# Thirteen column units of a mixer projection in full fp32, with unsplit weights and tokens

## The chip, the cores and the metric

The kernel runs on one core of one Trainium2 chip. The metric is device time in microseconds (us) of one execution. Of the kernel before there are three timed runs, from 2965.73 to 2970.14 us with a median of 2966.01 us, and one profiled execution.

## The reference, cut to what matters

The program is two transformer blocks on one sequence of 256 tokens with model width 2048, everything in float32. The first block (a sparse attention, an RWKV-7 recurrence and a mixture of 16 experts) is touched by the change only in how some small parameters are loaded. The second block projects the normalised tokens to 12288 columns and feeds three mixers and three gates from them:

```python
h = rmsnorm(x, norm1_g[l])
proj = h @ w_in[l]
uv, s5_in = proj[..., :o_a], proj[..., o_a:o_b]          # 2048 and 1024 columns
qkv = proj[..., o_b:o_c]                                 # 3 x 1024 columns
gates = sigmoid(proj[..., o_c:].reshape(bsz, seq, 3, 2048) + b_gate[l])
y_a = gmlp_mixer(uv, ...)
y_b = s5_mixer(s5_in, ...)       # 64 groups of 16 channels, 64 complex states each,
                                 # s_t = a * s_(t-1) + B u_t, y = Re(C s) + d u, then a glu
y_c = stick_breaking_attention(q, k, v)      # 8 heads of 128
x = x + sum(gates * (ys @ w_branch)) @ w_out
x = x + square(relu(rmsnorm(x) @ w_mlp_in)) @ w_mlp_out
return rmsnorm(x, final_g)
```

## The kernel before, in words

**Products.** Weights come from memory in chunks of 512 KB (128 partitions x 1024 floats), issued by SP into one of three buffers `raw`. To multiply with nearly full precision at the fast rate, both factors are split into two fp32r parts: ACT copies a chunk into `wh` (L208), DVE subtracts that from the chunk into `wl` (L209), both in `load_split`. A *column unit* is 256 columns of a projection: `ws_steps` (L237) takes for each of the 16 slices of the model width and each half of 128 columns three matmuls into PSUM, wh by token-high, wh by token-low and wl by token-high (tiles `hx` in the trace), each with 256 tokens as the moving side. So such a unit has 96 matmuls, 4 chunks and 4 splits. Other units (W and V) have the tokens stationary, 512 columns moving, and are not touched.

**Order of the second block's mixers.** ORDER2 (L1478) lists the units: U and W are the two halves of the gated MLP, C the input of the state space mixer (S5), V and Q the attention (a Q unit is two column units, one of queries and one of keys), G the first gates, E the gelu of the S5 result. While PE goes through them, two generators are advanced: the S5 states (`rest`) each 3.9 us of planned matmul time, and the chains of gMLP and attention each 0.52. Within an engine a scheduler then fixes one order of all instructions; each engine works through its own queue in that order.

**The S5 states** are 32 steps i, four for each of eight tables. A step runs: PE makes the drive (`mx`); DVE multiplies it by cosine and sine tables (L1980, L1981, from PSUM), adds and subtracts (L1982, L1983), and scans two halves of 128 tokens for real and imaginary part (four L1993, with three small ops L1989 to L1991 between the halves); POOL multiplies the states back (L1995, L1996, into `b` and `z`); `result` subtracts and adds (L2003, L2004) on DVE if `i % 4 < CO`, else on POOL; ACT rounds to `sh` (L2007), POOL makes `sl` (L2008), and PE multiplies both with `C` into the result. POOL also builds the tables (L1948 to L1953, seven doublings each).

**After the S5 states** come the glu of its result (tiles `gs`), the branch products, the output projection and the MLP, all split products.

**Parameters.** `late_params` runs at the start of the expert stage: six rows of parameters are loaded by POOL's queue into a buffer of its own (`parl_r`) and transposed on PE (L176).

Of the kernel before, what the change touches and what calls it, by code (L numbers as in the profile page):

```python
# [10 lines left out]
F32 = mybir.dt.float32  # L11
# [3 lines left out]
OP = mybir.AluOpType  # L15
# [3 lines left out]
T = 256  # L19
D = 2048  # L20
KD = D // 128
EC = math.exp(-0.5)
LB = 3
WB = 1024
# [4 lines left out]
def _consts():  # L29
    p = np.arange(128)[:, None]  # L30
    f = np.arange(128)[None, :]
    t = np.arange(T)[None, :]
    c = {}
    c["ident"] = p == f
    c["bd64"] = (p // 64) == (f // 64)
    for d in (128, 64):
        half = d // 2
        inv = np.float32(10000.0) ** (-np.arange(half, dtype=np.float32) * np.float32(2.0 / d))
        ang = np.arange(T, dtype=np.float32)[:, None] * inv.astype(np.float32)[None, :]
        cos = np.cos(ang).astype(np.float32).T  # L40
# [12 lines left out]
    c["blk"] = (p // b) == (f // b)  # L53
    c["nsel"] = np.where(p % b == f[:, :b], -1.0, 0.0)
    c["iota"] = np.broadcast_to(f, (128, 128))
    c["before"] = p < f
    c["geq"] = p >= f
    c["strict"] = p < f
    c["tril"] = p >= f
    c["ntril"] = np.where(p >= f, -1.0e30, 0.0)  # L60
# [9 lines left out]
C2 = ("iota", "before")  # L70
C3 = ("geq", "strict", "tril", "ntril", "half", "odd")

# [43 lines left out]
class Ker:  # L116
    def __init__(self, tc, A, out, stack, dbg=None):
        self.tc, self.nc, self.A, self.out, self.dbg = tc, tc.nc, A, out, dbg or {}
        self.ctx = stack
        self.glob = self.pool("glob", 1)  # L120
        self.rawp = self.pool("raw", 3)
        self.whp = self.pool("wh", 3)
        self.slots, self.only, self.nraw, self.ahead, self.pending = None, None, 0, [], None
        self.par, self.done = None, set()
        self.sides, self.nmx = False, 0
# [35 lines left out]

    def param_rows(self, items, pool, name, q=None):
        nc = self.nc
        n = sum(i[2] for i in items)
        assert n <= 128
        r = pool.tile([128, 128], F32, name=name + "_r", tag="prow")
        nc.vector.memset(r, 0.0)
# [22 lines left out]
    def load_raw(self, parts, kn, cn):  # L190
        raw = self.raw_tile()
        rv = raw[:, :kn * cn].rearrange("p (k c) -> p k c", k=kn)
        for ap, c0 in parts:
            w = ap.shape[1]
            self.nc.sync.dma_start(rv[:, :, c0:c0 + w], ap.rearrange("(k p) c -> p k c", p=128))
        return raw

    def load_split(self, parts, kn, cn):
# [37 lines left out]

    def ws_steps(self, parts, cn, xh, xl, pieces, kn_chunk=4):  # L237

# [12 lines left out]
        for k0 in range(0, K, kn_chunk):  # L251
            h, l = self.load_split([(ap[k0 * 128:(k0 + kn_chunk) * 128], c) for ap, c in parts],
                                   kn_chunk, cn)
            for k in range(kn_chunk):
# [75 lines left out]
    def columns(self, x, g):  # L330
# [6 lines left out]
        def quarter(q):  # L337
            for k in range(4 * q, 4 * q + 4):
                ps = self.pmx()
                for b in range(2):  # L340
                    nc.tensor.transpose(ps[:, ts(b, 128)], x[:, b, ts(k, 128)], self.ident)  # L341
                nc.scalar.activation(hh[:, k], ps[:, :T], AF.Copy, scale=g[:, k:k + 1])  # L342
                nc.vector.scalar_tensor_tensor(hl[:, k], ps[:, :T], g[:, k:k + 1],
                                               hh[:, k].bitcast(F32), op0=OP.mult, op1=OP.subtract)
        self.hx = [hx[:, k].rearrange("p a t -> p (a t)") for k in range(KD)]
        return quarter, [hh[:, k] for k in range(KD)], [hl[:, k] for k in range(KD)]
# [97 lines left out]
    def late_params(self):  # L444

        A = self.A
        row = lambda n: A[n].rearrange("l (r c) -> (l r) c", c=128)
# [4 lines left out]
            ("b_glu", [(row("s5_b_glu_2"), 0, 0)], 8), ("s5_d", [(row("s5_d_2"), 0, 0)], 8),  # L452
            ("gm_g", [(row("gm_norm_g_2"), 0, 0)], 8)], self.glob, "parl")

# [697 lines left out]
    def moe(self):  # L1152
        nc, A, tc = self.nc, self.A, self.tc
        stt = nc.vector.scalar_tensor_tensor
        with ExitStack() as st:
# [20 lines left out]
            with ExitStack() as s2:  # L1176
                q = self.pool("rt", 1, stack=s2)
                wr = q.tile([128, KD, 20], F32, name="wr")
                nc.gpsimd.dma_start(wr[:, :, 0:4], A["w_route_group"][0].rearrange("(k p) c -> p k c", p=128))
                nc.gpsimd.dma_start(wr[:, :, 4:20], A["w_route_expert"][0].rearrange("(k p) c -> p k c", p=128))  # L1180
                br = q.tile([128, 20], F32, name="br")
# [293 lines left out]
    EARLY, XB, SB = (4, 2, 1)  # L1475
    LO, CO = (0, 2)
    PRE = (0,)
    RS, RC = (3.9, 0.52)  # L1478
    ORDER2 = ('U0', 'C0', 'C1', 'U1', 'U2', 'W0', 'C2', 'C3', 'W1', 'U3', 'GM', 'G0', 'V0', 'Q0', 'Q1', 'V1', 'Q2', 'Q3', 'G1', 'G2', 'E', 'G3')

    def block2(self):
# [3 lines left out]
        with ExitStack() as st:  # L1485
# [11 lines left out]
            def gate(d, pool, n, ci):  # L1497

                g = d[n, ci] = pool.tile([128, 512], F32, name="g")
                c0 = 6144 + 2048 * n + 256 * ci  # L1500
                v, bk = yield from self.ws_steps([(w_in[:, c0:c0 + 256], 0)], 256, hh, hl, two)
                nc.vector.tensor_mul(*(t.rearrange("p (a t) -> p a t", a=2) for t in (g, bk[0])), row)
# [31 lines left out]
            with ExitStack() as s2:  # L1534
                early, steps, chains = {}, {}, []
                vp = self.pool("vv", 1, stack=s2)
                steps.update(self.gmlp(y, w_in, vp, chains))
                steps.update(self.sb(y, w_in, vp, chains))
# [5 lines left out]
                cs = cc = 0.0  # L1544
                for n in self.ORDER2:
                    for t in steps[n]():
                        cs += t
# [11 lines left out]
                for ch in chains:  # L1559
                    for _ in ch:  # L1560
                        pass
            q = self.pool("br", 1, stack=st)
            gq = self.pool("gq", 2, stack=st)
# [68 lines left out]
    def gmlp(self, y, w_in, vp, chains):  # L1632
# [9 lines left out]
        def U(j):  # L1642
            if j == 0:
                nc.gpsimd.dma_start(ws, A["gm_w_s_2"][0].rearrange("g t s -> t g s"))
                nc.gpsimd.tensor_mul(ws, ws, c["tril"][:, None, :].to_broadcast([128, 8, 128]))
                nc.gpsimd.dma_start(bs, A["gm_b_s_2"][0][None].to_broadcast([128, 8, 128]))
            v, bk = yield from self.ws_steps([(w_in[:, ts(j, 256)], 0)], 256, hh, hl, two)
            yj = y[:, 2 * j:2 * j + 2]
# [46 lines left out]
    def sb(self, y, w_in, vp, chains):  # L1695
# [18 lines left out]
        def attend(j):  # L1714
# [4 lines left out]
            for i, (base, sc) in enumerate(((3072, 128 ** -0.5), (4096, 1.0))):  # L1719
                v, bk = yield from self.ws_steps([(w_in[:, base + 256 * j:base + 256 * (j + 1)], 0)], 256, hh, hl, two)  # L1720
                nc.vector.scalar_tensor_tensor(both[:, 2 * i:2 * i + 2], bk[0].rearrange("p (a t) -> p a t", a=2), sc,
                                               self.row, op0=OP.mult, op1=OP.mult)
            chains.append(heads(j, both[:, 0:2], both[:, 2:4], pre))

        def heads(j, q, k, pre):
# [15 lines left out]
            for i, w in enumerate(work):  # L1741
# [5 lines left out]
                nc.vector.tensor_sub(zs, zs, cs[:, :384])  # L1747
                nc.vector.tensor_add(dg(zs), dg(zs), b2(c["ntril"]))
                with self.tc.issue_after(pre):
# [40 lines left out]
    def s5(self, y, w_in, st):  # L1790
# [6 lines left out]
        with ExitStack() as s1:  # L1797
# [71 lines left out]
            pat = "(s a) n h -> (a n) s h"  # L1869
            nc.gpsimd.dma_start(br, A["s5_b_re_2"][0].rearrange(pat, a=2))  # L1870
            nc.gpsimd.dma_start(bi, A["s5_b_im_2"][0].rearrange(pat, a=2))
            kb = lambda k: sc[:, k][:, :, None].to_broadcast([128, 32, 16])
# [16 lines left out]
        def cols(j):  # L1889
            v, bk = yield from self.ws_steps([(w_in[:, 2048 + 256 * j:2304 + 256 * j], 0)], 256, hh, hl, two)  # L1890
            yj = y[:, 8 + 2 * j:10 + 2 * j]
# [270 lines left out]
```

## Time and profile before

| what | value |
|---|---|
| median of three runs | 2966.01 us |
| profiled execution | 2965.45 us |
| its span, first to last instruction | 2963.3 us |
| mean granted clock of TensorE | 0.988 of full speed |
| busy: PE, DVE, ACT, POOL | 96%, 71%, 54%, 15% of the span |
| instructions on PE, DVE, ACT, POOL | 17284, 2898, 2161, 623 |

The profiled execution stands for the median: it is 0.02% below it, and 2.2 us of it lie outside the span. The shares are averages over stages. PE is near full in most of the 40 slices of the page; the second block's mixers, with the S5 states, are the slices from about 1300 to 1770 us, and there alone POOL is busy.

### The profile page before, as it was taken

How to read it: one execution, taken by the hardware profiler on the slowest of the kernel's cores; microseconds unless marked ns; L12 is line 12 of the kernel's file. 1: busy time of each engine (PE TensorE's matmuls, PEld its weight loads, DVE VectorE, ACT ScalarE, POOL GpSimd, SP SyncE). 2: the span in 40 equal slices, each digit the busy share in tenths (PEclk: the TensorE clock that was granted, in tenths of full speed). 3: DMA queues.
4: the chain of work that ended last, by engine and by line, in shares of the span. 5: the costliest groups of instructions: out<-in, count | busy, mean ns of one | idle time of the engine just before them, and what ended most of it. 6: DMA issues, size and time to landing. Idle time of an engine off the chain costs nothing. (4 is left out here: it accounts for less than half of the span.)

```text
span 2963.3 us, 45262 instructions
## 1 busy us (share of the span) xinstructions
PE 2854.0 (96%) x17284; PEld 2508.5 (85%) x17284; DVE 2105.6 (71%) x2898; ACT 1613.5 (54%) x2161; POOL 456.4 (15%) x623
## 2 busy tenths in 40 slices
PE   8999999997999999998888889999999999999998
PEld 8998989876887788787777779999988888888887
DVE  7685876647898989887999987555555654456554
ACT  6456466546777777765444445444445553345443
POOL 1211111011000000017998840000000000000000
PEclk9999999998999999999999999999999999999999
DMA  6444443484989999854434336665556666666665
GB/s 196 131 116 122 116 117 104 128 288 154 371 289 348 378 370 354 313 169 145 125 114 121 100 107 193 185 186 185 183 184 196 190 188 194 194 187 190 190 194 171
DMA packets 400512, 576.77 MB, mean 195 GB/s; under 512 B 25032, under 2 KB 252624, under 8 KB 400160
## 3 DMA queue, kind: packets, MB, share of 16 engines
q1 hardware_dynamic: 397632, 567.74, 59.5%
q0 software_dynamic: 2624, 6.06, 0.8%
q8 instruction: 137, 2.24, 0.3%
q14 instruction: 87, 0.71, 0.1%
q10 hardware_dynamic: 32, 0.01, 0.0%
HBM read 571.64 MB, written 2.10 MB: 194 GB/s over the span
## 5 line engine op out<-in xcount | busy, mean ns | idle before, releaser
L209 DVE TENSOR_TENSOR wl<-raw,wh 128x1024 fp32r<-128x1024 f32 (+1 forms) x917 | 1135.1, 1241 | 631.2 <-ACT wh L208 618.8
L208 ACT ACTIVATE wh<-raw 128x1024 fp32r<-128x1024 f32 (+1 forms) x917 | 965.6, 1055 | 908.7 <-PE acc L218 717.1
L218 PE MATMUL acc<-hx,wh 128*128 128x256 f32 (+3 forms) x5280 | 1163.5, 310 | 0.2 <-ACT hx L342 0.2
L218 PEld LDWEIGHTS acc<-hx,wh 128*128 128x128 f32 (+2 forms) x5280 | 862.0, 192 | 55.2 <-issue 8.5
L218 PE MATMUL acc<-hx,wl 128*128 128x256 f32 x3152 | 896.1, 286 | 11.2 <-DVE wl L209 11.1
L218 PEld LDWEIGHTS acc<-hx,wl 128*128 128x128 f32 x3152 | 602.0, 191 | 22.0 <-DVE wl L209 13.0
L209 DVE TENSOR_TENSOR wl<-rx,wh 128x1024 fp32r<-128x1024 f32 x159 | 191.9, 1225 | 29.9 <-ACT wh L208 26.7
L218 PE MATMUL acc<-wl,xgh 128*128 128x512 f32 x512 | 203.6, 399 | 2.3 <-DVE wl L209 2.3
L218 PE MATMUL acc<-wh,xgh 128*128 128x512 f32 x512 | 202.4, 396 | 2.4 <-ACT wh L208 2.4
L218 PE MATMUL acc<-wh,xgl 128*128 128x512 f32 x512 | 202.4, 395 | 0.0
L208 ACT ACTIVATE wh<-rx 128x1024 fp32r<-128x1024 f32 x159 | 167.5, 1060 | 59.5 <-PE acc L218 33.0
L218 PE MATMUL acc<-wh,al 128*128 128x512 f32 x512 | 199.3, 389 | 0.0
L218 PE MATMUL acc<-wh,ah 128*128 128x512 f32 x512 | 199.2, 389 | 0.0
L218 PE MATMUL acc<-wl,ah 128*128 128x512 f32 x512 | 179.2, 389 | 0.0
L218 PE MATMUL mx<-wh,act 128*128 128x512 f32 x512 | 141.2, 395 | 1.5 <-DVE act L215 0.8
L218 PE MATMUL acc<-wh,hx 128*128 128x512 f32 x384 | 123.9, 407 | 0.0
L218 PEld LDWEIGHTS acc<-wl,xgh 128*128 128x128 f32 x512 | 96.2, 188 | 27.0 <-DVE wl L209 4.8
L218 PEld LDWEIGHTS acc<-wh,xgh 128*128 128x128 f32 x512 | 96.2, 188 | 24.6 <-ACT wh L208 3.6
L218 PEld LDWEIGHTS mx<-wh,act 128*128 128x128 f32 x512 | 95.8, 188 | 25.1 <-DVE act L215 1.2
L218 PEld LDWEIGHTS acc<-wh,xgl 128*128 128x128 f32 x512 | 96.1, 188 | 22.3
L218 PEld LDWEIGHTS acc<-wh,ah 128*128 128x128 f32 x512 | 96.1, 188 | 20.0
L218 PEld LDWEIGHTS acc<-wl,ah 128*128 128x128 f32 x512 | 96.2, 188 | 19.9
(589 smaller groups left out, 4150.9 us busy)
## 6 DMA issues: line engine op xcount, KB each, us to landing
raw<-in_w_in_dram SPq DMA_DIRECT2D x304, 512.0 KB, 3.7
raw<-in_w_mlp_in_dram SPq DMA_DIRECT2D x128, 512.0 KB, 3.8
raw<-in_w_mlp_out_dram SPq DMA_DIRECT2D x128, 512.0 KB, 4.6
raw<-in_w_e_gate_dram SPq DMA_DIRECT2D x80, 512.0 KB, 6.0
raw<-in_w_e_down_dram SPq DMA_DIRECT2D x77, 512.0 KB, 5.7
raw<-in_w_e_up_dram SPq DMA_DIRECT2D x75, 512.0 KB, 5.6
raw<-in_w_out_dram SPq DMA_DIRECT2D x57, 512.0 KB, 3.8
rx<-in_w_e_up_dram SPq DMA_DIRECT2D x53, 512.0 KB, 6.4
```

What stands on the lines that cost most here:

```text
L208: self.lasth = nc.scalar.activation(h[:, :n], raw[:, :n], AF.Copy).ins
L209: self.lastl = nc.vector.tensor_sub(l[:, :n], raw[:, :n], h[:, :n].bitcast(F32)).ins
L218: return self.nc.tensor.matmul(out, lhsT, rhs, start=start, stop=stop)
```

## The change

Nine names of ORDER2, thirteen column units in all, multiply the chunk as it was loaded by unsplit tokens, one fp32 matmul in place of three fp32r ones. The chunks go in turn into the buffers that were `raw`, `wh` and `wl`, and no ACT or DVE instruction touches them. The tokens `xf` (16 KB a partition) are made by four additions on POOL. The room is found by: a GpSimd descriptor room of 2048 bytes in place of the size that is set when nothing is said (a few DMAs on its queue are cut into pieces for it), two constants less, and the parameter rows of `late_params` in a `raw` buffer. CO goes from 2 to 4, so all 32 pairs of L2003 and L2004 are on DVE.

```diff
-C3 = ("geq", "strict", "tril", "ntril", "half", "odd")
+C3 = ("geq", "strict", "half", "odd")
...
+    def load_direct(self, parts, kn, cn):
+        self.nhome = (self.nhome + 1) % 3
+        t = (self.rawp if self.nhome == 0 else self.whp).tile([128, WB], F32, name=("raw", "wh", "wl")[self.nhome])
+        v = t[:, :kn * cn].rearrange("p (k c) -> p k c", k=kn)
+        for ap, c0 in parts:
+            w = ap.shape[1]
+            self.nc.sync.dma_start(v[:, :, c0:c0 + w], ap.rearrange("(k p) c -> p k c", p=128))
+        return v
...
+            if xf is not None:
+                w = self.load_direct(rows, kn_chunk, cn)
+                for k in range(kn_chunk):
+                    kk = k0 + k
+                    for i, (c0, m) in enumerate(pieces):
+                        self.mm(views[i], w[:, k, c0:c0 + m], xf[:, kk], start=kk == 0 and first[i],
+                                stop=kk == K - 1 and last[i])
+                    yield 0.43 * len(pieces)
+                continue
...
     def late_params(self):
+        rows = self.raw_tile()[:, :128]
...
-                nc.gpsimd.dma_start(wr[:, :, 0:4], A["w_route_group"][0].rearrange("(k p) c -> p k c", p=128))
-                nc.gpsimd.dma_start(wr[:, :, 4:20], A["w_route_expert"][0].rearrange("(k p) c -> p k c", p=128))
+                for k in (0, 8):
+                    for n, c0, c1 in (("group", 0, 4), ("expert", 4, 20)):
+                        nc.gpsimd.dma_start(wr[:, k:k + 8, c0:c1], A["w_route_" + n][0, k * 128:(k + 8) * 128]
...
-    LO, CO = (0, 2)
+    LO, CO = (0, 4)
+    DIRECT = ("U2", "C2", "C3", "U3", "Q0", "Q1", "Q2", "Q3", "G1")
...
+                full = self.pool("xf", 1, stack=s2).tile([128, KD, T], F32, name="xf")
+                for k in range(0, KD, 4):
+                    a, b = (self.hxt[:, k:k + 4, i].bitcast(F32) for i in range(2))
+                    nc.gpsimd.tensor_add(full[:, k:k + 4], a, b)
...
+                    self.xf = full if n in self.DIRECT else None
...
-                nc.vector.tensor_add(dg(zs), dg(zs), b2(c["ntril"]))
+                nc.vector.scalar_tensor_tensor(dg(zs), b2(c["geq"]), -1.0e30, dg(zs), op0=OP.mult, op1=OP.add)
...
-            nc.gpsimd.dma_start(br, A["s5_b_re_2"][0].rearrange(pat, a=2))
-            nc.gpsimd.dma_start(bi, A["s5_b_im_2"][0].rearrange(pat, a=2))
+            for s in range(0, 32, 8):
+                for t_, n in ((br, "re"), (bi, "im")):
+                    nc.gpsimd.dma_start(t_[:, s:s + 8], A[f"s5_b_{n}_2"][0, 2 * s:2 * s + 16].rearrange(pat, a=2))
...
-    nc = bacc.Bacc("TRN2", target_bir_lowering=False, num_devices=1)
+    nc = bacc.Bacc("TRN2", target_bir_lowering=False, num_devices=1, dynamic_dma_scratch_size=2048)
```

The scheduler orders the queues anew. First DVE, in the middle of the S5 scans, as it was before (`wl<-raw,wh` is a split, `z<-sc,a` a scan):

```order
L209 TENSOR_TENSOR wl<-raw,wh 128x1024
L215 TENSOR_TENSOR Bl_17378<-mx,Bh_17377 128x256
L1993 SCALAR_TENSOR_TENSOR z<-sc,a_17465 128x128 x2
L1993 SCALAR_TENSOR_TENSOR z<-sc,a_17313 128x128 x2
L209 TENSOR_TENSOR wl<-raw,wh 128x1024
L1938 TENSOR_TENSOR C_13630<-mx,C_13630 128x2x32 x2
L1989 SCALAR_TENSOR_TENSOR a_17465<-z,eh,a_17465 128x2
L1980 TENSOR_TENSOR a_17598<-mx,tab 128x512
L1981 TENSOR_TENSOR a_17599<-mx,tab 128x512
L1990 SCALAR_TENSOR_TENSOR a_17465<-z,eh,a_17465 128x1
L1991 SCALAR_TENSOR_TENSOR a_17465<-z,eh,a_17465 128x1
L209 TENSOR_TENSOR wl<-raw,wh 128x1024
```

And DVE near the end of the scans now (the lines of the S5 steps stand 30 lower in the file, L1980 is L2010):

```order
L2010 TENSOR_TENSOR a_17067<-mx,tab 128x512
L2011 TENSOR_TENSOR a_17068<-mx,tab 128x512
L2050 TENSOR_TENSOR y_13453<-y_13453,mx 64x256
L2020 SCALAR_TENSOR_TENSOR a_17012<-z,eh,a_17012 128x1
L2021 SCALAR_TENSOR_TENSOR a_17012<-z,eh,a_17012 128x1
L2012 TENSOR_TENSOR a_17067<-a_17067,a_17068 128x256
L2013 TENSOR_TENSOR a_17067<-a_17067,a_17068 128x256
L2023 SCALAR_TENSOR_TENSOR z<-sc,a_17012 128x128 x2
L2033 TENSOR_TENSOR b_16949<-b_16949,z 128x256
L2034 TENSOR_TENSOR b_16949<-b_16949,z 128x256
```

From the first scan to the last, 81 splits stood among them before and 29 stand there now; the pairs on `b` are all in this queue.

On PE, at the end of the S5 states, before, `mx<-sl,C` is the last product of the last step, and 93 more split matmuls like those behind it come before the glu:

```order
L218 MATMUL acc<-hx,wl 128x256
L218 MATMUL mx<-sl,C_13629 128x256
L218 MATMUL mx<-sh,C_13630 128x256
L218 MATMUL mx<-sl,C_13630 128x256
L218 MATMUL acc<-hx,wh 128x256 x2
L218 MATMUL acc<-hx,wl 128x256
```

And now, in the same place:

```order
L226 MATMUL mx<-sl,C_13645 128x256
L226 MATMUL mx<-sh,C_13646 128x256
L226 MATMUL mx<-sl,C_13646 128x256
L226 MATMUL acc<-xf,wh 128x256 x5
L226 MATMUL acc<-xf,wl 128x256 x8
L226 MATMUL acc<-xf,raw 128x256
L226 MATMUL mx<-zsb,cst_c_13438 128x256
```

Behind the last S5 product there now stand 29 fp32 matmuls, the rest of the last attention heads and 288 split matmuls (three units) before the glu begins; the S5 states end earlier in PE's order.

On PE, at the start of the expert stage, in the output projection of the first block (`yx`), now (`raw` is the buffer with the parameter rows):

```order
L226 MATMUL acc<-wh,yx 128x512
L226 MATMUL acc<-wl,yx 128x512
L174 MATMUL mx<-cst_cg,raw 128x128
L226 MATMUL acc<-wh,yx 128x512 x8
L226 MATMUL acc<-wl,yx 128x512
```

and before, further down the same projection:

```order
L218 MATMUL acc<-wl,yx 128x512
L218 MATMUL acc<-wh,yx 128x512 x2
L218 MATMUL acc<-wl,yx 128x512
L176 MATMUL mx<-cst_cg,parl_r 128x128
L1192 MATMUL mx<-cst_cg,xr 128x128 x2
L218 MATMUL acc<-wl,yx 128x512
```

The transposition of the parameter rows has moved up: twelve `yx` matmuls now stand between the last product of the recurrence (`PT,V`) and it.

## Rows read from the trace of the kernel before

**Rows 1.** The page's first part: busy time, share of the span, instructions.
```profile
PE 2854.0 (96%) x17284; PEld 2508.5 (85%) x17284; DVE 2105.6 (71%) x2898; ACT 1613.5 (54%) x2161; POOL 456.4 (15%) x623
```

**Rows 2.** A window behind the stage: start and end, length, busy time of each engine, PEclk, DMA, GB/s.
```profile
1800.00:1900.00 100.00, 100.00 (x843) 100.00 (x843) 58.40 (x60) 43.44 (x49) 0.00 (x0) 1.00 0.61 188
```

**Rows 3.** Windows by stage, from the third U unit to the last S5 result.
```profile
1332.00:1392.00 60.00, 53.95 (x344) 47.44 (x343) 44.86 (x88) 34.74 (x62) 48.54 (x99) 0.98 0.52 154
1392.00:1764.00 372.00, 316.56 (x2025) 283.00 (x2026) 351.48 (x575) 159.76 (x264) 304.63 (x389) 0.94 0.38 114
```

**Rows 4.** Waits of PE, 1392 to 1764: microseconds in total, times, longest.
```profile
PE mx L218 <- POOL sl L2008: 17.4, 13, 3.1
PE acc L218 <- DVE wl L209: 13.0, 7, 7.3
```

**Rows 5.** DVE by line, 1392 to 1764: count | busy, mean ns | idle before, releaser.
```profile
L209 DVE TENSOR_TENSOR wl<-raw,wh 128x1024 fp32r<-128x1024 f32 x80 | 115.9, 1451 | 4.9 <-ACT wh L208 4.7
L1993 DVE TENSOR_TENSOR_SCAN z<-sc,a 128x128 f32<-128x128 f32 x120 | 71.5, 632 | 0.1
L2004 DVE TENSOR_TENSOR b<-b,z 128x256 f32<-128x256 f32 x15 | 9.1, 608 | 0.0
L2003 DVE TENSOR_TENSOR b<-b,z 128x256 f32<-128x256 f32 x15 | 7.6, 504 | 9.1 <-POOL z L1996 9.1
```

**Rows 6.** POOL by line, the same stretch.
```profile
L2008 POOL TENSOR_TENSOR sl<-b,sh 128x512 fp32r<-128x512 f32 x32 | 48.0, 1501 | 22.3 <-ACT sh L2007 22.3
L2004 POOL TENSOR_TENSOR b<-b,z 128x256 f32<-128x256 f32 x16 | 16.9, 1058 | 0.0
L2003 POOL TENSOR_TENSOR b<-b,z 128x256 f32<-128x256 f32 x16 | 14.9, 933 | 1.1
```

**Rows 7.** DVE in order of time: start, microseconds, instruction.
```profile
1689.75 1.44 DVE L1993 TENSOR_TENSOR_SCAN z<-sc,a 128x128 f32<-128x128 f32 x1
1696.32 1.21 DVE L209 TENSOR_TENSOR wl<-raw,wh 128x1024 fp32r<-128x1024 f32 x1
1699.65 0.73 DVE L1993 TENSOR_TENSOR_SCAN z<-sc,a 128x128 f32<-128x128 f32 x2
```

**Rows 8.** PE in order of time, an fp32 pair and three fp32r products.
```profile
1578.33 0.89 PE L218 MATMUL mx<-sqk 128*128 128x256 f32 x4 [0.55 <-DVE a L1981]
1578.98 0.36 PE L218 MATMUL acc<-hx,wh 128*128 128x256 f32 x1
1579.18 0.28 PE L218 MATMUL acc<-hx,wl 128*128 128x256 f32 x1
1579.53 0.28 PE L218 MATMUL acc<-hx,wl 128*128 128x256 f32 x1
```

**Rows 9.** The last S5 product on PE, and the glu tiles' first matmul.
```profile
1765.33 0.28 PE L218 MATMUL mx<-sl,C 128*128 128x256 f32 x1
...
L218 PE MATMUL acc<-gs,wh x128: 276/279/331, 1776.6 to 1799.9; 128*128 128x256 f32 x128
```

**Rows 10.** POOL's parameter loads, a landing time (last column), and PE in that place.
```profile
605.33 0.56 POOL L145 DMA_DIRECT2D cst_c<-in_c_dram  x1 [88.08 <-ACT yx L214]
608.88 0.50 POOL L172 DMA_DIRECT2D parl_r<-in_gm_norm_g_dram  x1
...
parl_r<-in_gm_norm_g_dram POOLq DMA_DIRECT2D x1, 4.0 KB, 5.1
...
608.01 0.84 PE L218 MATMUL acc<-wh,yx 128*128 128x512 f32 x3
637.87 0.27 PE L176 MATMUL mx<-cst_cg,parl_r 128*128 128x128 f32 x1
```

**Rows 11.** A window after PE's longest wait in the S5 stretch.
```profile
1389.00:1403.00 14.00, 8.98 (x39) 8.43 (x39) 13.57 (x24) 4.57 (x9) 7.56 (x7) 0.51 0.38 108
```

**Rows 12.** POOL before the tables: the last long operation, and the wait behind it.
```profile
1295.59 2.40 POOL L1645 TENSOR_TENSOR gv<-gv,cst_c 128x1024 f32<-128x1024 f32 x1 [6.90 <-DMA gv<-in_gm_w_s_dram]
1341.26 0.95 POOL L1882 DMA_DIRECT2D cc<-in_s_c_re_dram  x1 [43.27 <-DVE eh L1865]
```

More of the change, by code (lines that the diff above doesn't have):

```diff
@@ L58, in _consts @@
     c["strict"] = p < f
-    c["tril"] = p >= f
-    c["ntril"] = np.where(p >= f, -1.0e30, 0.0)
     c["half"] = (p // 64) == np.arange(2)[None, :]
@@ L124, in __init__ @@
         self.par, self.done = None, set()
-        self.sides, self.nmx = False, 0
+        self.sides, self.nmx, self.nhome = False, 0, 0
         self.acc = self.pool("acc", 4, PSUM)
@@ L160, in pmx, with param_rows @@
         return self.mx.tile([128, 512], F32, name="mx", tag="mx", bufs=3)
-    def param_rows(self, items, pool, name, q=None):
+    def param_rows(self, items, pool, name, q=None, rows=None):
         nc = self.nc
@@ L165, in param_rows @@
         assert n <= 128
-        r = pool.tile([128, 128], F32, name=name + "_r", tag="prow")
+        r = pool.tile([128, 128], F32, name=name + "_r", tag="prow") if rows is None else rows
         nc.vector.memset(r, 0.0)
@@ L235, in ts_group, with ws_steps @@
         return self.whole(self.ts_steps(*args, **kw))
-    def ws_steps(self, parts, cn, xh, xl, pieces, kn_chunk=4):
+    def ws_steps(self, parts, cn, xh, xl, pieces, kn_chunk=4, xf=None):
         K = len(xh)
@@ L251, in ws_steps @@
         for k0 in range(0, K, kn_chunk):
-            h, l = self.load_split([(ap[k0 * 128:(k0 + kn_chunk) * 128], c) for ap, c in parts],
-                                   kn_chunk, cn)
+            rows = [(ap[k0 * 128:(k0 + kn_chunk) * 128], c) for ap, c in parts]
+            if xf is not None:
[7 more added lines that the diff above has]
+                continue
+            h, l = self.load_split(rows, kn_chunk, cn)
             for k in range(kn_chunk):
@@ L344, in quarter @@
                                                hh[:, k].bitcast(F32), op0=OP.mult, op1=OP.subtract)
+        self.hxt = hx
         self.hx = [hx[:, k].rearrange("p a t -> p (a t)") for k in range(KD)]
@@ L452, in late_params @@
             ("b_glu", [(row("s5_b_glu_2"), 0, 0)], 8), ("s5_d", [(row("s5_d_2"), 0, 0)], 8),
-            ("gm_g", [(row("gm_norm_g_2"), 0, 0)], 8)], self.glob, "parl")
+            ("gm_g", [(row("gm_norm_g_2"), 0, 0)], 8)], self.glob, "parl", rows=rows)
     def dump(self, name, t):
@@ L1178, in moe @@
                 wr = q.tile([128, KD, 20], F32, name="wr")
-                nc.gpsimd.dma_start(wr[:, :, 0:4], A["w_route_group"][0].rearrange("(k p) c -> p k c", p=128))
-                nc.gpsimd.dma_start(wr[:, :, 4:20], A["w_route_expert"][0].rearrange("(k p) c -> p k c", p=128))
+                for k in (0, 8):
+                    for n, c0, c1 in (("group", 0, 4), ("expert", 4, 20)):
+                        nc.gpsimd.dma_start(wr[:, k:k + 8, c0:c1], A["w_route_" + n][0, k * 128:(k + 8) * 128]
+                                            .rearrange("(k p) c -> p k c", p=128))
                 br = q.tile([128, 20], F32, name="br")
@@ L1500, in gate @@
                 c0 = 6144 + 2048 * n + 256 * ci
-                v, bk = yield from self.ws_steps([(w_in[:, c0:c0 + 256], 0)], 256, hh, hl, two)
+                v, bk = yield from self.ws_steps([(w_in[:, c0:c0 + 256], 0)], 256, hh, hl, two, xf=self.xf)
                 nc.vector.tensor_mul(*(t.rearrange("p (a t) -> p a t", a=2) for t in (g, bk[0])), row)
@@ L1561, in block2 @@
                         pass
+            self.xf = None
             q = self.pool("br", 1, stack=st)
@@ L1644, in U @@
                 nc.gpsimd.dma_start(ws, A["gm_w_s_2"][0].rearrange("g t s -> t g s"))
-                nc.gpsimd.tensor_mul(ws, ws, c["tril"][:, None, :].to_broadcast([128, 8, 128]))
+                nc.gpsimd.tensor_mul(ws, ws, c["geq"][:, None, :].to_broadcast([128, 8, 128]))
                 nc.gpsimd.dma_start(bs, A["gm_b_s_2"][0][None].to_broadcast([128, 8, 128]))
-            v, bk = yield from self.ws_steps([(w_in[:, ts(j, 256)], 0)], 256, hh, hl, two)
+            v, bk = yield from self.ws_steps([(w_in[:, ts(j, 256)], 0)], 256, hh, hl, two, xf=self.xf)
             yj = y[:, 2 * j:2 * j + 2]
@@ L1719, in attend @@
             for i, (base, sc) in enumerate(((3072, 128 ** -0.5), (4096, 1.0))):
-                v, bk = yield from self.ws_steps([(w_in[:, base + 256 * j:base + 256 * (j + 1)], 0)], 256, hh, hl, two)
+                v, bk = yield from self.ws_steps([(w_in[:, base + 256 * j:base + 256 * (j + 1)], 0)], 256, hh, hl, two, xf=self.xf)
                 nc.vector.scalar_tensor_tensor(both[:, 2 * i:2 * i + 2], bk[0].rearrange("p (a t) -> p a t", a=2), sc,
@@ L1889, in cols @@
         def cols(j):
-            v, bk = yield from self.ws_steps([(w_in[:, 2048 + 256 * j:2304 + 256 * j], 0)], 256, hh, hl, two)
+            v, bk = yield from self.ws_steps([(w_in[:, 2048 + 256 * j:2304 + 256 * j], 0)], 256, hh, hl, two, xf=self.xf)
             yj = y[:, 8 + 2 * j:10 + 2 * j]
```

## The prediction

> **What bounds the kernel now.** I read the page's first part, then windows, then the waits of PE in the windows that are not full, then the lines of DVE and POOL there. The first part shows PE busy 96% and DVE 71% of the span [rows 1]: as a mean, a PE-bound kernel. The windows show the exception. Behind the mixers PE is busy in 100 of 100 us and POOL in none [rows 2]; from 1392 to 1764, the 372 us in which the S5 scans run, PE is busy 316.6, DVE 351.5 (94.5%) and POOL 304.6 [rows 3]. There PE waits for `sl` (17.4 us, made by POOL) and for `wl` (13.0 us, made by DVE) [rows 4]: for the end of the S5 chain and for splits that queue on DVE among S5 operations. And its granted clock is 0.94 [rows 3], since after the longest of these waits, 7.3 us [rows 4], a window of 14 us ran at 0.51, the lower of the two levels [rows 11]. So DVE bounds this stretch, with POOL close, and PE the rest. I follow three sums: PE's work, DVE's work in the stretch, and what stands behind the stretch.
>
> **PE: dearer by about 33 us.** Thirteen units of 16 slices and two halves are 416 products of 256 columns. As three fp32r matmuls one costs 0.35 us: two `wl` matmuls one product apart start at 1579.18 and 1579.53 [rows 8]. An fp32 product's price stands just above: four records from 1578.33, the next matmul at 1578.98, 0.65 us [rows 8]. In that tile an fp32 matmul leaves two records, so these are one of 256 and one of 128 columns, and 256 columns cost 0.65 x 256/384 = 0.43 us. 416 x (0.43 - 0.35) = 33 us. By the start of the next fp32r record the bounds are 0.075 and 0.10 a product, 31 to 41 us. In a stretch that PE bounds this is lost; in one that DVE bounds it goes into PE's idle time, 372 - 317 = 55 us.
>
> The two passes of each fp32 product load weights twice, and the row says this is hidden, since the 0.65 us hold four loads as well [rows 8]. [...]
>
> **DVE: cheaper by about 57 us in the stretch.** 52 splits go, some three of them ahead of 1392; of 80 in the stretch I take 49 off. One costs 1.21 us where nothing disturbs it [rows 7] and 1.45 in the mean [rows 5]: 59 to 71 us; I take 71, since those left out were disturbed like the others. POOL's 32 operations of the pairs (16.9 + 14.9 us) [rows 6] come to DVE, where they cost 0.56 in the mean of the two lines [rows 5]: +18, or +13 at an undisturbed price of about 0.4. DVE's operations are long when POOL works beside them: a scan alone took 1.44 us, two together 0.73 [rows 7], and the mean is 0.632 [rows 5], so 120 scans lose 120 x 0.27 = 32 us. POOL's load falls from 305 to 273, a tenth, so I take 4 us off for this. DVE then has 351.5 - 71 + 18 - 4 = 294 us; at the same 94.5% the stretch takes 311 us and ends at 1703 in place of 1764. That is 10.0 us for each of 31 steps where it was 12.0. The bounds: at undisturbed prices throughout and all delays gone (-59, +13, -32) 274, so 290 us; with nothing gained, 372.
>
> [...]
>
> The stretch starts as before: its first operation waits for POOL's tables, and POOL for DVE's `eh` up to 1341 [rows 12]. The four additions for `xf`, 2.4 us each by POOL's operation of the same size, stand in the 43 us in which POOL waits there [rows 12], as do the eight pieces of `br` and `bi`. The first direct unit needs `xf` at about 1332; from 1298 there are 34 us for 10 us of work. If the smaller descriptor room makes each piece wait for the one before, 5 us each by a landing of that queue [rows 10], eight take 40 in place of a few, and `xf` is some 5 to 15 us late: a bound of +15, of which I take 0.
>
> **Behind the stretch PE has more left.** Before, 93 split matmuls stood between the last S5 product (1765.3) and the glu (1776.6) [rows 9]. Now 29 fp32 products (12.5 us), the last heads of the attention (2048 columns, 3.4 us, with their waits 7) and 288 split matmuls (288 x 0.118 = 34) stand there: 53.6 us. The last S5 product comes at 1704.5, the glu at 1758: 18.6 us earlier. A gain of 61 on DVE's side thus pays 19, since the PE work that used to fill the stretch now follows it. What is left from 1776.6 to the end is unchanged.
>
> **At the expert stage about 8 us are lost.** The parameter rows lie in a `raw` buffer now, and their transposition on PE stands twelve matmuls behind the end of the recurrence, in place of some 30 us later (637.87) [rows 10]. Twelve end at 608.0, where PE went on before. But POOL issues the loads from 605.33, since it waited there, the last at 608.88, and that one takes 5.1 us to land [rows 10]: 614. PE waits 6 us, with the whole projection behind it. A slow clock behind such a pause cost 14 x 0.49 = 7 us after 7.3 us [rows 11]; this one is shorter, and I take 2, between 0 and 7. Sum +8, from 0 (if the buffer and the loads are earlier) to 13.
>
> **The sum** from the profiled execution's 2965.45 us (0.02% under the median, so nothing is corrected): -18.6 + 8 = -10.6, so 2955 us. It is near break-even: with a stretch of 321 us in place of 311 nothing is gained.
>
> **The rivals.**
>
> *PE bounds the mixers.* If the chain no longer holds PE, the time from 1332 to 1776.6 is PE's work: 54 + 316.6 + 11.3 [rows 3, 9], 382 us busy of 444.6, plus 33 is 415; without waits the clock stays up, and the 6% of 372 us that it lacked are won back, 22 us: 393. The glu starts at 1725, 51 us earlier; with +8 it is 2922. If the clock does not come back, 2944. For it speaks that PE waits for `wl` in just the places where splits are gone now; against it, that each step's operations still go in turn through DVE, POOL, ACT and PE, and that POOL has 273 us of work.
>
> *The chain keeps its pace: slower.* If the 12.0 us of a step are the turn-around between DVE and POOL and not DVE's work, then fewer splits only leave DVE idle. Then the S5 states end at 1765 as now, 53.6 us follow, the glu is at 1819, and with +8 the time is 3016. In the trace 22.3 us of POOL's idle time ended with ACT's `sh` [rows 6] and 9.1 of DVE's with POOL's `z` [rows 5], which speaks for some turn-around; that DVE is 94.5% busy [rows 3] speaks against it. The price falls with each us that a step gets shorter: 31 steps at 10.35 us are break-even, above that it is slower.
>
> *Late tokens.* The pieces of `br` and `bi` wait for room, `xf` comes 15 us late, and PE stands still before the first direct unit and runs on at the lower clock: 2955 + 15 + 7 = 2977, about 0.4% slower than before. For it speaks only the landing time; against it the 34 us of room.
>
> *The direct loads don't hide.* That the transfers bound is excluded: the same bytes are loaded, at 114 GB/s in the stretch against 188 behind it [rows 2, 3].
>
> **How the numbers follow.** This kernel's runs can tell about 0.2%, 6 us, from no change. The forecast's own case (a stretch of 303 to 321 us) gets 0.45, from 2947 to 2965; PE-bound 0.22, from 2922 to 2947; the slower chain 0.23, from 2965 to 3016, most of it below 2985, since each us won on DVE counts; late tokens 0.10. Faster by over 0.2% (below 2960) is the second case and three quarters of the first: 0.56. Within 0.2% are a quarter of the first and a third of the third: 0.19. Slower, with the late tokens: 0.25. The range that leaves out 2 in 10 is 2922 to 2985; the forecast's own is 2947 to 2965.
>
> **What would show it.** In the changed profile: the fp32 products start 0.43 us apart; DVE's splits between the scans number about 31 and POOL has no `b` pairs; the stretch from the first to the last scan lasts about 311 us, with DVE over 90% busy; from the last `mx<-sl,C` to the first `gs` matmul pass some 54 us; PE waits about 6 us for a parameter load near 608; behind the glu nothing is different. Wrong would be: DVE below 85% in the stretch while its length stays over 321 (then the turn-around sets the pace), PE over 97% busy there (then PE bounds it), a wait of PE for `xf` near 1332, or fp32 products clearly above 0.43 us.

## The result

| kernel | median us | runs | ratio to before, 95% interval |
|---|---|---|---|
| before | 2965.87 (2964.49 to 2970.14) | 4 | |
| changed | 3008.86 (3003.53 to 3011.34) | 4 | 1.0139 (1.0122 to 1.0155) |

The change makes the kernel 43 us slower; 2955 us was forecast, from 2922 to 2985. The profiled execution of the changed kernel has a span of 3001.6 us, 38.3 us over before, and the comparison below is of these two executions.

The page's first part, against [rows 1]: DVE has 57 us less to do, as the change says, POOL 64 us less, and PE 30 us more.

```profile
PE 2883.9 (96%) x16868; PEld 2512.2 (84%) x16868; DVE 2049.0 (68%) x2878; ACT 1562.3 (52%) x2109; POOL 392.4 (13%) x603
```

To find where the time went I read the start of the same work in both traces. The columns after "before" and "changed" are the start of the instruction, and the last column is what was added since the line above.

| place | before | changed | added |
|---|---|---|---|
| end of the recurrence, first `yx` matmul behind it | 605.1 | 604.1 | -1.0 |
| first expert matmul (`acc<-wh,xgh`) | 695.0 | 724.8 | +30.8 |
| last expert matmul (`mx<-wh,act`) | 1273.4 | 1304.5 | +1.3 |
| first glu matmul (`acc<-gs,wh`) | 1776.6 | 1815.9 | +8.2 |
| end of the span | 2963.3 | 3001.6 | -1.0 |

So four fifths of the loss stand in the 90 us between the recurrence and the experts, where nothing is computed in another way, and the rest in the mixers, where 19 us less were forecast.

**Ahead of the experts.** PE in order of time (start, duration, instruction, idle time before it and what ended it), and ACT's first copy there:

```profile
608.95 0.63 PE L226 MATMUL acc<-wl,yx 128*128 128x512 f32 x1
612.83 0.42 PE L174 MATMUL mx<-cst_cg,raw 128*128 128x128 f32 x1 [3.25 <-DMA raw<-in_gm_norm_g_dram]
635.65 3.78 PE L226 MATMUL acc<-wh,yx 128*128 128x512 f32 x8 [22.40 <-ACT wh L216]
...
634.54 1.06 ACT L216 ACTIVATE wh<-raw 128x1024 fp32r<-128x1024 f32 x1 [29.88 <-DMA raw<-in_w_out_dram]
```

Where PE ran on before [rows 10], it now waits 3.25 us for the parameter rows and then 22.40 us for a copy of ACT, which had waited 29.88 us for a chunk of `w_out`. SP's queue shows why that chunk is late: first the changed kernel, then the one load that before has in between.

```profile
582.21 3.16 SPq L408 DMA_DIRECT2D raw<-in_x_dram  x2
603.61 0.37 SPq L193 DMA_DIRECT2D rx<-in_w_out_dram  x1
604.03 0.46 SPq L408 DMA_DIRECT2D rx<-in_x_dram  x1
604.54 3.33 SPq L193 DMA_DIRECT2D rx<-in_w_out_dram  x6
607.92 2.91 SPq L193 DMA_DIRECT2D raw<-in_w_out_dram  x2
611.22 0.85 SPq L408 DMA_DIRECT2D raw<-in_x_dram  x1
612.56 11.07 SPq L193 DMA_DIRECT2D raw<-in_w_out_dram  x8
```

```profile
584.94 0.37 SPq L195 DMA_DIRECT2D raw<-in_w_out_dram  x1
```

Before, the chunk was issued at 584.94, as soon as its buffer was free (a split on DVE ended at 584.92). Now the parameter rows lie in that buffer. In SP's order the load now stands behind eighteen others: it is the last of nineteen transfers from 603.61 on (the eighth of those from 612.56), and it waits for PE's transposition of the rows (`PE_49`):

```
before: L195 DMA raw<-in_w_out_dram 128x2x512 [waits DMAHW6_49,DVE_49]
changed: L193 DMA raw<-in_w_out_dram 128x2x512 [waits DMASW5_49,DMASW4_49,DMASW6_49,DMASW3_49,DMASW7_49,DMASW1_49,DMAHW3_49,DMASW0_49,PE_49]
```

It is issued near 623.6 (612.56 and 11.07), behind eighteen transfers of 512 KB, and ACT can begin at 634.54. The transposition itself had ended near 613.25 (612.83 and 0.42), some ten us before the load was issued: what makes the load late is its place in SP's order.

**In the mixers, ahead of the S5 steps.** POOL, DVE and PE at one time:

```profile
1344.82 9.37 POOL L1563 TENSOR_TENSOR xf<-hx 128x1024 f32<-128x1024 f32 x4
1354.15 2.33 POOL L1674 TENSOR_TENSOR gv<-gv,cst_c 128x1024 f32<-128x1024 f32 x1
...
1344.03 12.53 DVE L1812 TENSOR_SCALAR xmq<-xmq 32x128 f32<-32x128 f32 x1
...
1359.42 0.50 PE L1880 MATMUL mx<-cst_cg,pk 32*128 32x32 f32 x3 [8.84 <-DVE pk L1840]
```

A DVE instruction on 32x128 elements, 0.2 us elsewhere in the same line, lasts 12.53 us: from 1344.03 to 1356.56, until POOL is through the four additions for `xf` and one product (1344.82 to 1356.48). By its record it begins 0.79 us before the first addition, while POOL issues a load (1344.24 to 1344.80); whether that issue holds it too is not shown. What follows on DVE is late, and PE waits 8.84 us for it. Before, beside the product alone [rows 12] (1295.59 to 1297.99), an instruction whose line takes 0.16 us in the median lasted until 1298.01:

```profile
1296.04 1.97 DVE L1783 TENSOR_SCALAR xdq<-xdq 32x2 f32<-32x2 f32 x1
```

**In the S5 stretch.** The windows from the first `sl` to the last scans' results, to be held against [rows 3], and DVE and POOL by line in the first of them, against [rows 5, 6]:

```profile
1424.00:1747.00 323.00, 290.52 (x1401) 241.27 (x1400) 278.25 (x542) 99.83 (x194) 233.02 (x357) 0.96 0.36 111
1747.00:1816.00 69.00, 67.22 (x453) 63.21 (x452) 28.79 (x37) 32.12 (x51) 2.53 (x2) 1.00 0.40 123
```

```profile
L2023 DVE TENSOR_TENSOR_SCAN z<-sc,a 128x128 f32<-128x128 f32 x120 | 62.3, 562 | 0.1
L217 DVE TENSOR_TENSOR wl<-raw,wh 128x1024 fp32r<-128x1024 f32 x28 | 40.3, 1440 | 3.4 <-ACT wh L216 3.2 <-DVE xin L1930 0.2
L2010 DVE TENSOR_TENSOR a<-mx,tab 128x512 f32<-128x512 f32 x28 | 19.0, 679 | 9.0 <-PE mx L226 8.9
L2034 DVE TENSOR_TENSOR b<-b,z 128x256 f32<-128x256 f32 x32 | 22.1, 690 | 0.0
L2033 DVE TENSOR_TENSOR b<-b,z 128x256 f32<-128x256 f32 x32 | 18.1, 566 | 19.6 <-POOL z L2026 19.5
...
L2025 POOL TENSOR_TENSOR b<-z,tab 128x512 f32<-128x512 f32 x30 | 42.1, 1402 | 65.5 <-DVE z L2023 61.5 <-DVE a L2019 3.1 <-DVE vr L326 0.8
```

DVE's work fell somewhat further than forecast: 28 splits where 80 were (31 were forecast), all 32 pairs, 278 us busy (294 were forecast). But it is busy 86% of the stretch, not 94.5%. It waits 19.5 us for POOL's `z` (9.1 before [rows 5]), and now also 19.3 us in all for products of PE (8.9 of them in the line of L2010), where before there were 1.3. POOL waits 61.5 us for DVE's scans. From the first `b` of POOL to the last `z` pass 320 us (1419.4 to 1738.9), 370 before (1386.3 to 1756.7). PE is busy 90% of the stretch, 85% before [rows 3].

And behind it (PE, the last S5 product and the fp32 products after it; then the first glu matmul):

```profile
1759.65 0.28 PE L226 MATMUL mx<-sl,C 128*128 128x256 f32 x1
1759.77 2.32 PE L226 MATMUL acc<-xf,wh 128*128 128x256 f32 x10
1761.93 1.24 PE L226 MATMUL acc<-xf,wl 128*128 128x256 f32 x5
...
L226 PE MATMUL acc<-gs,wh x128: 279/280/282, 1815.9 to 1838.3; 128*128 128x256 f32 x128
```

From the last S5 product to the glu pass 56.3 us, where 53.6 were forecast and 11.3 stood before [rows 9]. Ten records, five fp32 products, take 2.16 us from 1759.77: 0.43 us each, as priced.

### The profile page after: what moved, and what is told of

It reads as the page before. It is cut to its first block, busy times and chain, and to the rows that moved or that the text cites. A ratio compares the mean times of both kernels' runs of the same rounds, so it can differ in the third digit from the quotient of the medians.

```text
span 3001.6 us, 44257 instructions
## 1 busy us (share of the span) xinstructions
PE 2883.9 (96%) x16868; PEld 2512.2 (84%) x16868; DVE 2049.0 (68%) x2878; ACT 1562.3 (52%) x2109; POOL 392.4 (13%) x603
## 4 chain that ended last, share of the span: by engine, by line
PE 46%; DVE 6%; POOL 4%; issue 1%; DMA 1%; ACT 0%; SPq 0%; ACTq 0%; DVEq 0%; POOLq 0%
PE acc L226 44%; PE mx L226 1%; DVE z L2023 1%; POOL b L2025 1%; POOL z L2026 1%; DVE xmq L1812 0%; POOL sl L2038 0%; POOL tab L1980 0%; DVE b L2034 0%; POOL ttmp L1979 0%; POOL tab L1978 0%; POOL tab L1981 0%; DVE wl L217 0%; POOL ttmp L1982 0%; POOL tab L1983 0%
## 5 line engine op out<-in xcount | busy, mean ns | idle before, releaser
L217 DVE TENSOR_TENSOR wl<-raw,wh 128x1024 fp32r<-128x1024 f32 (+1 forms) x865 | 1058.8, 1227 | 668.5 <-ACT wh L216 656.5
L216 ACT ACTIVATE wh<-raw 128x1024 fp32r<-128x1024 f32 (+1 forms) x865 | 911.0, 1055 | 939.3 <-PE acc L226 697.0
L226 PE MATMUL acc<-hx,wh 128*128 128x256 f32 (+3 forms) x4448 | 1000.6, 313 | 1.2 <-ACT wh L216 0.8
L226 PE MATMUL acc<-hx,wl 128*128 128x256 f32 x2736 | 773.0, 285 | 1.5 <-DVE wl L217 1.4
L226 PEld LDWEIGHTS acc<-hx,wh 128*128 128x128 f32 (+2 forms) x4448 | 724.9, 190 | 55.8 <-issue 8.0
L226 PEld LDWEIGHTS acc<-hx,wl 128*128 128x128 f32 x2736 | 518.7, 190 | 10.7 <-issue 4.5
L226 PEld LDWEIGHTS acc<-wh,al 128*128 128x128 f32 x512 | 96.1, 188 | 20.0
```

What stands on the lines that cost most here:

```text
L216: self.lasth = nc.scalar.activation(h[:, :n], raw[:, :n], AF.Copy).ins
L217: self.lastl = nc.vector.tensor_sub(l[:, :n], raw[:, :n], h[:, :n].bitcast(F32)).ins
L226: return self.nc.tensor.matmul(out, lhsT, rhs, start=start, stop=stop)
```

## The experiments

All times are medians, with the ratio to the kernel before as it ran on the same chip and its 95% interval. "Experts" is the start of the first expert matmul (695.0 before), "mixers" the time from the last expert matmul to the first glu matmul (503.2 before).

| kernel | us | ratio, interval | experts | mixers |
|---|---|---|---|---|
| changed | 3008.9 | 1.0139 (1.0122 to 1.0155) | 724.8 | 511.4 |
| rows moved | 2985.5 | 1.0070 (1.0053 to 1.0087) | 700.8 | 515.7 |
| additions on DVE | 2997.2 | 1.0113 (1.0096 to 1.0130) | 723.5 | 504.1 |
| br, bi by ACT | 3006.2 | 1.0142 (1.0126 to 1.0159) | 725.6 | 514.7 |
| rows moved, additions on DVE ("both") | 2972.3 | 1.0021 (1.0011 to 1.0030) | 701.9 | 504.0 |
| before, rows in `raw` | 2996.3 | 1.0107 (1.0091 to 1.0124) | 726.2 | 501.7 |
| both, no unit direct | 2973.4 | 1.0030 (1.0018 to 1.0041) | 700.9 | 501.2 |
| both, 4 units direct | 2967.8 | 1.0008 (0.9998 to 1.0018) | 700.7 | 498.6 |
| both, CO 2 | 2967.3 | 1.0007 (0.9997 to 1.0017) | 700.0 | 499.5 |
| both, CO 2, wr by ACT | 2971.1 | 1.0021 (1.0012 to 1.0030) | 704.6 | 499.8 |
| the same, 4 units direct | 2971.0 | 1.0016 (1.0007 to 1.0025) | 706.7 | 498.3 |
| rows in their own buffer, additions on DVE, CO 2 | 2961.9 | 0.9986 (0.9977 to 0.9995) | 696.5 | 499.4 |
| the same, 4 units direct | 2961.8 | 0.9987 (0.9978 to 0.9996) | 695.3 | 498.1 |

My theories: A, the raw buffer with the parameter rows is needed for the next chunk, and that costs the 30 us ahead of the experts; X, the POOL additions in a row hold up DVE; P, in the S5 stretch DVE and PE weigh about the same, so what fp32 takes from the one it gives to the other. The rivals: B, only the transposition waits; R, the small descriptor room makes the S5 parameters late; D, the relief of DVE is worth the forecast 19 us; N, fp32 only costs.

**The rows out of the raw buffer.**

```diff
-            self.late_params()
+            self.late_params(raw2.tile([128, WB], F32, name="raw")[:, :128])
```

> The changed kernel with the parameter rows in a buffer of the expert stage instead of a raw buffer. Theory A (the raw buffer with the rows is the one that the next chunk of the first block's output projection needs, so that chunk is loaded behind 17 others and PE waits 22 us for it, besides 3 us for the rows): the first expert matmul starts near 695 us as before, and the time falls by 28 to 33 us, from 3009 to about 2978. Rival B (what costs is only the transposition that waits for the rows, 3.2 us, and the slow clock behind it): it falls by at most 8 us, to about 3001.

The time fell by 23 us to 2985.5, less than the 28 to 33 that A gave, and the expert matmuls started at 700.8, not near 695. Both waits are gone, and the chunk was issued at 584.90 again. So A held for the waits, and B (at most 8 us) did not; 5 to 6 us of the loss stayed, which the last experiments take up.

**The same place in the kernel before.** One edit to it: `rows=self.raw_tile()[:, :128]` in `late_params`.

> The kernel before with one edit: the parameter rows in a raw buffer, as in the changed kernel. Theory A (the raw buffer with the rows is needed for the next chunk of the output projection): all of what this edit costs is in the first block's output projection, PE waits 20 us and more for a chunk near 613 us, and the time is 23 to 31 us above before, 2989 to 2997. Rival B (only the transposition waits): at most 8 us, 2974.

It cost 30.6 us. PE's waits from 600 to 700 (total, times, longest):

```profile
PE acc L218 <- ACT wh L208: 24.0, 1, 24.0
PE mx L176 <- DMA raw<-in_gm_norm_g_dram: 6.1, 1, 6.1
```

The wait for the transposition that I had priced is 6.1 us, as I had it; the wait for the chunk, which I had not, is 24.0 us.

**The additions on DVE.** `nc.vector.tensor_add` in place of `nc.gpsimd.tensor_add` for `xf`.

> The changed kernel with the four additions that make the unsplit tokens on DVE instead of POOL. Theory X (five long POOL operations in a row keep one small DVE instruction from 1344.0 to 1356.6, and PE waits 8.8 us behind it, then runs on a slow clock): no DVE instruction of the S5 parameters takes over 3 us, PE's wait near 1359 is gone, and the time falls by 9 to 14 us, to about 2997. Rival R (the S5 parameters are late since the eight pieces of br and bi wait for the small descriptor room, to 1340): the wait stays, and the time is within 3 us of 3009.

2997.2 us, 11.7 less, and PE is busy without a gap where it waited, at full clock. The last piece of `bi` is still issued only at 1338.89, so the late pieces that R names are there and the wait is not:

```profile
1330.00:1364.00 34.00, 34.00 (x279) 33.42 (x279) 28.83 (x84) 13.58 (x15) 7.15 (x6) 1.00 0.75 224
```

**br and bi by ACT's queue**, whole, in place of eight pieces that are issued 3.2 to 4.4 us apart.

```diff
-            for s in range(0, 32, 8):
-                for t_, n in ((br, "re"), (bi, "im")):
-                    nc.gpsimd.dma_start(t_[:, s:s + 8], ...)
+            nc.scalar.dma_start(br, A["s5_b_re_2"][0].rearrange(pat, a=2))
+            nc.scalar.dma_start(bi, A["s5_b_im_2"][0].rearrange(pat, a=2))
```

> The changed kernel with br and bi loaded whole by ACT's queue, not in eight pieces by POOL's. Rival R (the room makes them late): the wait of PE near 1359 is gone and the time falls by 9 to 14 us, to about 2997. Theory X: the POOL additions come some 25 us earlier but still stand in a row, one small DVE instruction still takes about 10 us beside them, and the time falls by 0 to 6 us, since the S5 chain may then be less late.

2.7 us less, which the spread of the runs (3003.5 to 3011.3 before the edit, 3005.8 to 3010.6 with it) cannot tell from nothing, so R fell here too. In detail it went another way than X had it: two additions and the product stand in a row, the other two additions each alone, and three DVE instructions last until the POOL operations beside them end, 5.33, 2.32 and 2.39 us. First POOL, then DVE:

```profile
1315.69 4.75 POOL L1563 TENSOR_TENSOR xf<-hx 128x1024 f32<-128x1024 f32 x2
1320.41 2.33 POOL L1674 TENSOR_TENSOR gv<-gv,cst_c 128x1024 f32<-128x1024 f32 x1
1327.20 3.35 POOL L1563 TENSOR_TENSOR xf<-hx 128x1024 f32<-128x1024 f32 x1 [4.45 <-DVE xdf L1808]
...
1317.56 5.33 DVE L1865 TENSOR_TENSOR den<-lre 32x128 f32<-32x128 f32 x1
1328.25 2.32 DVE L1809 TENSOR_SCALAR xdq<-xdf 32x2 f32<-32x2 f32 x1
```

PE's wait moved with them (5.7 us for a DVE `hx`). In all three kernels that were run with the additions on POOL, one of these small instructions was that long (12.53, 12.13 and 5.33 us).

**Both edits.**

> The changed kernel with both edits: rows in a buffer of the expert stage, and the additions on DVE. Theories A and X together: 28 to 33 and 9 to 14 us less, 2962 to 2972, about the time of the kernel before (2966). If only A is right about 2978, if only X about 2997, if neither over 3000.

2972.3 us: A and X together, 36.6 us, just past the end of what was expected. The mixers take 504.0 us, and 503.2 in the kernel before: with both waits mended, the 13 fp32 units and the 32 pairs on DVE together gain nothing.

**Both edits, and no unit direct** (`DIRECT = ()`).

> The changed kernel with the rows in a buffer of the expert stage and the additions on DVE (2972 us, as the run with both edits), and now with no unit direct: all 28 column units split, all 32 pairs of the S5 on DVE. What the fp32 products are worth by themselves. Theory P (DVE bounds the S5 stretch, and what the fp32 products take off it is given back by PE, whose work grows by 33 us): the S5 states end 40 us and more later, but only a few matmuls follow them, and the time is within 8 us of 2972. Rival D (DVE's relief is worth the forecast 19 us and something else lost it): 2985 to 2995. Rival N (the fp32 products only cost): below 2960.

2973.4 us, within 1.1 of the run with 13 units: P. The last S5 product comes 52 us later (500.1 us after the last expert matmul, 448.3 with 13 units, and 1.1 us ahead of the glu). The mixers as one window, with 13 units and with none:

```profile
1282.40:1786.40 504.00, 461.07 (x2497) 394.71 (x2496) 404.48 (x800) 188.43 (x350) 292.00 (x470) 0.97 0.42 127
```

```profile
1279.50:1780.70 501.20, 443.28 (x2913) 399.39 (x2913) 459.24 (x845) 233.38 (x389) 329.63 (x470) 0.95 0.43 128
```

DVE is busy 404 us in place of 459. PE is busy 461 in place of 443, and idle 43 in place of 58: 15 us less idle, 18 us more work (33 were priced at full clock; the granted clock is 0.97 with 13 units and 0.95 with none).

What DVE waits for between the first `b` and the last `z`, with 13 units (328.9 us, 1388.2 to 1717.1) and then with none (371.8 us, 1400.1 to 1771.9):

```profile
DVE b L2033 <- POOL z L2026: 15.5, 6, 5.4
DVE a L2010 <- PE mx L226: 9.7, 4, 4.7
DVE zsb L1776 <- PE mx L226: 7.3, 1, 7.3
```

```profile
DVE b L2033 <- POOL z L2026: 15.1, 9, 2.9
DVE y L2050 <- PE mx L226: 2.2, 1, 2.2
```

The waits for POOL are the same. Those for PE are 19.4 us in all with 13 units and 2.2 with none: the engine that was relieved now waits for the one that got the work. DVE is busy 87% of the stretch with 13 units, 94% with none. POOL's waits for DVE's scans are 59.0 and 56.0 us (32.2 in the kernel before), so they were there without a direct unit.

**4 of the 13 units direct**, DVE and PE between the two ends.

> As the run with both edits (2972 us), with only U2, C2, C3 and U3 direct, 4 units of 13. Theory P: PE's extra work falls from 33 to 10 us, DVE keeps 36 splits more than with 13 units, the stretch ends between the two, and the sum is better than either end if DVE and PE are about equally loaded: 2962 to 2972. Rival D: a part of the relief, 2978 to 2985.

2967.8 us, 4.5 better than 13 units, inside what P expected; PE is busy 443 us as with none. But the stretch does not end between the two: it is 375 us long (1385.0 to 1760.2), as with none, since 74 of the 80 splits are still in it. It only starts earlier, 106 us after the last expert matmul in place of 121.

**CO back at 2.**

> As the run with both edits (2972 us), with CO back at 2: half of the 32 pairs of subtractions and additions on POOL again. If DVE bounds the stretch with 13 units direct, 16 pairs at 0.63 us each, 20 us, come off DVE and POOL gets 32 us: a shorter stretch by up to 10 us, 2962 to 2972. If POOL or the turn-around between DVE and POOL sets the step, it is slower: 2975 to 2990.

2967.3 us: the 16 pairs on DVE cost 5.0 us. That was not asked in the prediction, which put them into DVE's sum. The time is where the first case had it, but its reason failed: the stretch is as long as with CO 4 (327.8 us for 328.9), DVE is busy in it 281 us for 285, and POOL 262 for 243. The second case, a step set by POOL or by the turn-around, asked for a slower kernel and failed too. What is gained stands behind the last S5 product (51.0 us to the glu in place of 55.7); why is not shown.

**The router weights by ACT's queue** (`nc.scalar.dma_start`, two pieces), on top of both edits and CO 2, with 13 and with 4 units:

> The changed kernel with rows in a buffer of the expert stage, additions on DVE, CO at 2, and the router weights wr loaded by ACT's queue in two pieces, not by POOL's in four that wait 6 us for each other. If the small descriptor room is what is left of the loss ahead of the experts (the first expert matmul at 700 us, at 695 before), that 5 us goes: 2961 to 2964, 2 to 5 us under before. If not, 2967 as without this edit.

> As e9_wr with only U2, C2, C3 and U3 direct. Theory P (DVE and PE weigh about the same in the S5 stretch; 13 units load PE by 33 us, 4 units by 10): between 2955 and 2964, at least as fast as with 13 units. If the relief of DVE counts for more, slower than with 13 units by 5 us.

Both times missed: 2971.1 us, 3.8 above the run without this edit, and 2971.0 (for 4 units with CO 2 no run without it was made). That 4 units are as fast as 13 held. The experts start later, not earlier; with 13 units there is a longer wait for a chunk of the projection at its end:

```profile
658.66 2.08 PE L226 MATMUL acc<-wh,yx 128*128 128x512 f32 x4 [4.15 <-ACT wh L216]
```

So taking the four pieces away did not bring the last 5 us back; the next runs do so with the four pieces in place. How the two transfers by ACT's queue delay that chunk was not tried.

**The rows in a buffer of their own**, as before the change; 64 bytes a partition were missing, and the descriptor room gave them (1984 bytes).

> As the run with both edits and CO at 2 (2967 us), but the parameter rows in a buffer of their own as in the kernel before (64 bytes of the descriptor room pay for what it lacks). Theory G (what is left of the loss ahead of the experts, the first expert matmul at 700 us against 695, is the buffer that the rows take from the ring of the expert stage, so that chunks of the projection come later): 694 to 697 us there, and 2961 to 2964. Rival W (the router weights in four pieces by POOL, 6 us apart): 2967 as before.

> As e11_own with only U2, C2, C3 and U3 direct, 4 units of 13: the mixers as with 4 units, which by theory P (DVE and PE about equally loaded) are within 4 us of 13 units: 2958 to 2966.

The experts start at 696.5 and 695.3, and the times are 2961.9 and 2961.8 us, the first 5.4 under the run with the rows in the expert stage's ring: G. These two are the only versions faster than the kernel before, by 0.14% (0.05 to 0.23%) and 0.13%, and whether 13 or 4 units are direct makes no difference that can be measured. Their mixers take 499.4 and 498.1 us, 503.2 before, so with CO at 2 the direct units may be worth some 4 us. A run with these edits and no unit direct was not made, so this is not shown.

## Why the prediction was wrong

**The loss ahead of the experts was mis-sized; this is the largest failure.** The step "Sum +8, from 0 ... to 13" counted PE's wait for the rows: six microseconds, and the kernel before with that one edit shows 6.1. It left out that the buffer has a next tenant. The same order of the queues that showed the transposition moved up shows that tenant's load behind eighteen others on SP, and the bound of 13 was worked out without looking at it. Measured: 30.6 us with the edit alone, 24.0 of them PE's wait for the next chunk.

**"Late tokens" was priced at nothing in the sum, and its mechanism was another one.** The prediction put the additions into POOL's idle time, and let PE wait for `xf` if they came late. PE never waited for `xf`: the additions end at 1354.15, and the first fp32 product starts at 1373.8. That POOL is idle says nothing on DVE, and the row that would have shown it stood in the trace: an instruction of DVE, 0.16 us in the median of its line, took 1.97 us beside the one POOL product in that place. Measured: 11.7 us, and 13.2 with the rows moved. The pieces that the rival named do come 3.2 to 4.4 us apart, the last at 1339.8, but the runs show no time that hangs on it. In the changed kernel's trace one DVE instruction, which by its record began 0.79 us before them, lasted 12.53 us, until five POOL operations in a row had ended.

**The S5 stretch: DVE's sum nearly held, its busy share did not.** 294 us of DVE work were forecast, and 275 (changed) and 285 (both edits) were measured from the first `b` to the last `z`. But the step "at the same 94.5%" failed: DVE is busy 86% and 87% of 320 and 329 us. The prediction kept DVE's idle share as it was, and put the 33 us of fp32 work into PE's idle time at no price. The runs with 13 units and with none show the price: DVE's waits for PE went from 2.2 to 19.4 us, while those for POOL stayed at 15. So it is not the turn-around between DVE and POOL that took what was missing. The sign that the prediction named for it (DVE below 85% with a length over 321) is not met in either kernel, and with CO back at 2 the stretch did not get longer, as it should have. In all kernels with 13 units the last `z` comes 433 to 440 us after the last expert matmul, whether the first `b` came 106 us after it (both edits: 434.7) or 115 (changed: 434.4). That points at PE's order of products as what sets the end. No run varied that order, so this stays argued.

In the terms of the forecast, the run with both edits against the kernel before: the stretch starts 7.1 us earlier and is 41.5 us shorter (61 were forecast), from its end to the last S5 product pass 5.0 us more (nothing was put there), and 44.4 us more PE work follows (42.3 were forecast). That is 0.8 us later at the glu, where 18.6 earlier were forecast. In the changed kernel, with the DVE instruction of 12.53 us, the four are +2.0, -50.9, +12.2 and +44.9, or 8.2 us later.

**PE's price and what follows the stretch held.** 0.43 us a product; the ten weight loads of the first five lie beside their matmuls (2.03 us from 1759.65, and the matmuls from 1759.77); 56 us behind the last S5 product for 54. The point of the forecast that most of a shorter stretch is paid back behind it was right as an account; the break-even that it named, 321 us, lies beside the 320 and 329 measured. What I did not see is how flat this is: with 0, 4 and 13 direct units and CO 4 the times lie within 6 us.

**The rivals.** PE did not come to bound the mixers alone (it is busy 90% of the stretch), nor did the chain keep its 12.0 us a step (329/31 is 10.6). That the kernel got slower is the sign of the third case, but it came from other places than the one it named: 22.8 of the us missed lie ahead of the experts, and 26.8 in the mixers.

## What to carry to other kernels

When a tile moves into a buffer of a ring, look for the ring's next tenant: when its load was issued before, in which row of its queue it stands now, and what is in that queue ahead of it. An operation put into an engine's idle time is free only if the engines beside it do not slow down (here a DVE instruction, 0.21 us in the median of its line, took 12.53 beside five POOL operations): look for a place in the trace where the same engine ran such an operation, and read what the others did then. And before work is moved from one of two nearly full engines to the other, sum both: here 15 us of PE's idle time went and 18 us of PE's work came, and the relieved DVE waited 17 us more for PE.

## What the runs showed of the hardware

Beside five POOL operations with no gap between them (1344.82 to 1356.48) one DVE instruction of 32x128 elements with a single tensor input lasted 12.53 us, to 1356.56 (12.13 us in the run with the rows moved). With the additions on DVE the six instructions of that line and form took 0.21 to 0.24 us. Where two and one stood in a row and two alone, three DVE instructions ended with the POOL operations beside them, after 5.33, 2.32 and 2.39 us. Behind two longer waits of PE in the changed kernel the granted clock was about half of full speed: 0.52 from 1359 to 1364, behind 8.84 us of idle time, then 1.00 from 1364 to 1372; 0.50 from 635 to 640, behind 22.40 us, then 1.00 from 641 to 700.
